# The last four gate outputs of the second token half, computed with the tokens stationary

## The chip, the cores and the metric

The kernel runs on one core of a Trainium2 chip. The metric is the device time of one execution in microseconds (us); lower is better. The profile calls the engines PE (TensorE, matmuls), PEld (the loading of its stationary operand, which overlaps PE), DVE (VectorE), ACT (ScalarE), POOL (GpSimd) and SP (the queue that issues DMAs here). SBUF is the on-chip memory with 128 partitions, PSUM the eight accumulation banks of 128 x 512 floats that PE writes.

## The reference

One layer of a hybrid decoder in float32, for one sequence of S = 1024 tokens and D = 1024 channels: an input projection with a pooling mixer and a gated recurrence, an output projection, an MLP with squared ReLU, and then a gated per-layer embedding (256 channels) and a final norm. Only the end matters here:

```python
z = rms_norm(h, norm_ple_g[l])
gate = jax.nn.sigmoid(z @ w_ple_gate[l] + b_ple_gate[l])
h = h + gate * (p[l] @ w_ple_proj[l])
return rms_norm(h, norm_final_g)
```

`rms_norm` divides each token's row by the root of the mean of its squares over the 1024 channels (plus 1e-6) and multiplies by a gain for each channel.

## The kernel before

Everything is held transposed: `H[o]` is a tile of 128 channels (partitions) by 1024 tokens, for o = 0 to 7. `FIRST` and `SECOND` are the first and second 512 tokens. Each float32 product is made of three matmuls over operands split into a high and a low part (`split`: ACT copies the high part, DVE subtracts it); in `mm` the stationary operand is a 128 x 128 block of weights and the tokens stream through as columns, taken in an interleaved order (`turns`; `got` and `by` undo it at the reading).

The gate stage is the end of the kernel. `GROUPS` names four groups of tokens, `ORDER` the outputs o in each: group 0 is `FIRST` with all eight outputs, group 1 is `SECOND` with outputs 2, 3, 4, 5, and groups 2 and 3 are the two halves of 256 tokens of `SECOND` with outputs 6, 7, 0, 1. For each output `ple_gate` makes 24 matmuls into one PSUM bank (8 blocks of channels, 3 products), `ple_proj` six into another (256 embedding channels), and `ple_out` reads both: sigmoid with the bias on ACT, multiply and add to `H[o]` on DVE, then the square on ACT (`Norm.add`) and its addition to an accumulator on DVE. `ple_psum` takes the two banks in turn from a pool of double banks (`banks`) and a pool of four single banks (`bank`, shared with the sums of the norms). The sums over channels for the final norm run over partitions, so they are matmuls with a matrix of ones (`Norm.sums`); `rstd` takes the root on ACT and the reciprocal on DVE. `finish` scales `H[o]` and stores four outputs at a time: the first half's during group 1, the 512:768 tokens' during group 3. The last 256 tokens end in `ple_last`: their outputs are scaled by the channel gain (`gain`) and transposed in 32 x 32 blocks on DVE (`turned`) so that the root of a token stands in a partition, and the last output's chain is written out step by step in cuts of 128 tokens, with three stores.

The weights of outputs 0 to 3 are loaded and split in the order of `FETCH` into two rotating pairs of tiles, so those of 0 and 1 are loaded again for the later groups; those of outputs 4 to 7 are split once, during group 0, into `B[4:]` in the space of `a_all`. `Z` (eight tiles, space "ple") holds the first half's normed and split tokens, `a_pair(k, 48)` the second half's.

The order on each engine comes from a planner: it places an instruction as soon as it takes its inputs to be ready, in program order among those that are. `pin`, while `in_order` is set, ties an instruction behind the one written before it on its engine; `ple_last` is pinned throughout. All DMAs of this stage go through SP's one queue, in order.

Of the kernel before, what the change touches and what calls it, by code (L numbers as in the profile page):

```python
# [7 lines left out]
F32 = mybir.dt.float32  # L8
# [5 lines left out]
P = 128  # L14
# [21 lines left out]
FRONT, BACK = (0, 1, 2, 3), (4, 5, 6, 7)  # L36
FETCH = ((0, 1, 2, 3), (), (0, 1), ())
# [21 lines left out]
def block_kernel(  # L59
# [4 lines left out]
    vec: bass.AP,  # L64
    w_lru: bass.AP,
# [42 lines left out]
    def pairs(tiles):  # L108
        return list(zip(tiles[::2], tiles[1::2]))
# [867 lines left out]
    Z, ple = [], []  # L977

    def open_ple():
        leave("s2")  # L980
        leave("wd")
        tiles = space("ple", 10, F32R)
        small[:] = tiles[8:]
        Z[:] = pairs(tiles[:8])
# [29 lines left out]
    gate_p, held = {}, []  # L1014
    root = pool.tile([P, 1], F32, name="root")
# [9 lines left out]

    def ple_gate(g, hs, o, pg, held=False):
        if o in FETCH[g]:
            gate_p[o] = weights()
        whi, wlo = gate_p[o]
        for k in range(NT):  # L1030
            zhi, zlo = z3(k, hs)
            mm(
                [(slice(0, hs.stop - hs.start), pg)], kblk(whi, k), kblk(wlo, k), zhi, zlo,
                k == 0, k == NT - 1, held=held and k == 0,
            )
# [18 lines left out]
    n_end = NT * (S - GROUPS[-1].start)  # L1054
    out_v = out[:, : NT * S - n_end].rearrange("p (o s) -> p o s", o=NT)
    out_end = out[:, NT * S - n_end :].rearrange("p (b x) -> p b x", b=n_end // S * 4)
    turned_all = t_all[:, 1:3].rearrange("p a s -> p (a s)").rearrange("p (b o j) -> p b o j", o=NT, j=32)
    turned_flat = t_all[:, 1:3].rearrange("p a s -> p (a s)").rearrange("p (b x) -> p b x", x=32 * NT)

    def store(os, hs):  # L1060
        nc.sync.dma_start(out_v[:, os, hs], h_all[:, os, hs])

    def finish(hs, os):

        if 0 in os:
            fin.rstd(rfin, fin.sums((hs,)))
        if hs != FIRST:
            for o in os[::4]:
                x = h_all[:, o : o + 4, hs]
                n = hs.stop - hs.start  # L1070
                nc.vector.tensor_tensor(x, x, rfin[:, hs].unsqueeze(1).broadcast_to([P, 4, n]), ALU.mult)
                store(slice(o, o + 4), hs)
            return
        for o in os:
            hv = H[o][:, hs]
            nc.vector.scalar_tensor_tensor(hv, hv, col("g_fin", o), rfin[:, hs], ALU.mult, ALU.mult)
            if o % 4 == 3:
                store(slice(o - 3, o + 1), hs)

    def gain(o, hs):  # L1080
        return nc.scalar.activation(H[o][:, hs], H[o][:, hs], AF.Identity, scale=col("g_fin", o))

    def turned(o, src=None):
        src = H[o][:, GROUPS[-1]] if src is None else src
        return nc.vector.transpose(turned_all[:, :, o], src)

    def ple_last(hs, prev, o, pg, pj):

        n = hs.stop - hs.start
        m = n // 2  # L1090
        t, e = (T[3 + i % 2][:, :n] for i in (o, o + 1))
        before, own = (T[3 + i][:, HALF : HALF + n] for i in range(2))
        scaled = T[3][:, HALF + n :][:, :n]
        hv = H[o][:, hs]
        cuts = slice(0, m), slice(m, n)
        in_order[:] = [True]
        pin(nc.scalar.activation(before, H[prev][:, hs], AF.Square))
        pin(gain(prev, hs))
        pin(nc.scalar.activation(by(t, pg), got(pg), AF.Sigmoid, bias=col("b_ple", o)))
        pin(nc.scalar.activation(root, t[:, :1], AF.Sqrt))  # L1100
        pin(turned(prev))
        pin(nc.vector.tensor_tensor(by(e, pj), by(t, pj), got(pj), ALU.mult))
        sums = [bank(f"n3_ps{hs.start}_{i}")[:, :m] for i in range(2)]
        for x, cut in zip(sums, cuts):
            for i, sq in enumerate((T[0][:, hs], before)):
                nc.tensor.matmul(x, ones_f, sq[:, cut], start=i == 0, stop=False)
        for x, cut in zip(sums, cuts):
            pin(nc.vector.tensor_tensor(hv[:, cut], hv[:, cut], e[:, cut], ALU.add))
            pin(nc.vector.tensor_tensor(own[:, cut], hv[:, cut], hv[:, cut], ALU.mult))
            nc.tensor.matmul(x, ones_f, own[:, cut], start=False, stop=True)  # L1110
        pin(nc.scalar.activation(scaled, hv, AF.Identity, scale=col("g_fin", o)))

        few = spread[:, 16:24]

        def roots(i):
            r = rfin[:, hs][:, cuts[i]]
            pin(nc.vector.transpose(r, sums[i]))
            x = few[:, 4 * i : 4 * i + 4]
            pin(nc.scalar.activation(x, r.rearrange("p (b t) -> p b t", t=32)[:, :, 0], AF.Sqrt, bias=eps, scale=1.0 / D))
            return x  # L1120

        def inverse(x):
            pin(nc.vector.reciprocal(x, x))

        def on_act(b):
            x = turned_flat[:, b]
            pin(nc.scalar.activation(x, x, AF.Identity, scale=few[:, b : b + 1]))

        def on_dve(b):
            x = turned_flat[:, b]  # L1130
            pin(nc.vector.tensor_scalar_mul(x, x, few[:, b : b + 1]))  # L1131

        def leave_for(bs):
            nc.sync.dma_start(out_end[:, bs], turned_flat[:, bs])

        a = roots(0)
        pin(turned(o, scaled))
        inverse(a)
        on_dve(0)
        on_act(1)  # L1140
        leave_for(slice(0, 2))
        b = roots(1)
        on_dve(2)
        on_act(3)
        leave_for(slice(2, 4))
        inverse(b)
        on_act(6)
        on_dve(4)
        on_dve(5)
        on_dve(7)  # L1150
        leave_for(slice(4, 8))
        in_order.clear()

    END = len(GROUPS) - 1
    for g, hs in enumerate(GROUPS):
        last = len(ORDER[g]) - 1
        if g == 1:
            fin.tmp = T[3:5]
        if g == END:
            fin.n[hs.start] = len(ORDER[1])  # L1160
        for n, o in enumerate(ORDER[g]):
            end = g == END and n == last
            pg, pj = ple_psum(g, hs, o, end)
            if g == 0 and n < 2:
                ple_gate(g, hs, o, pg, n == 1)
                held.append((o, pg, pj))
                if n == 0:
                    first_sums()
                    continue
                for o, pg, pj in held:  # L1170
                    ple_proj(hs, o, pj)
                for o, pg, pj in held:
                    ple_out(hs, o, pg, pj)
            elif end:
                ple_gate(g, hs, o, pg)
                ple_proj(hs, o, pj)
            else:
                ple_proj(hs, o, pj)
                if g == END and n == 1:
                    finish(GROUPS[END - 1], FRONT)  # L1180
                ple_gate(g, hs, o, pg)
            if g == 0 and 1 <= n < 5:
                raw = wp.tile([P, S], F32, tag="raw", name=f"wg0_{n + 3}_raw")
                nc.sync.dma_start(raw, w_gate[n + 3])
                split(raw, *B[n + 3])
                gate_p[n + 3] = B[n + 3]

            if (g > 0 or n > 1) and not end:
                ple_out(hs, o, pg, pj, g < END or n < last - 1)
# [7 lines left out]
            if g == 1:  # L1197
                gain(o, hs)
                finish(FIRST, DONE[n])
            if g == END - 1:  # L1200
                gain(o, hs)
                turned(ORDER[1][n])
            if g == END and n < last - 1:
                gain(o, hs)
                turned(o)
            if g == END and n == 1:
                finish(GROUPS[END - 1], BACK)
            if end:
                ple_last(hs, ORDER[g][n - 1], o, pg, pj)
    leave("ple")  # L1210
# [75 lines left out]
```

## Time and profile before

| what | value |
|---|---|
| median of 3 runs | 923.79 us (923.67 to 924.34) |
| the profiled execution | 923.81 us, of which 922.0 us are the span from first to last instruction |
| granted PE clock | 0.999 |
| PE busy | 914.2 us, 4357 matmuls |
| DVE busy | 760.3 us |
| ACT busy | 457.9 us |
| group 1 on PE | about 860.4 to 886.3 us |
| groups 2 and 3 on PE | about 886.3 to 913.5 us |
| from the last projection matmul to the end | about 8.5 us |

How to read the lines quoted below: a line of the timeline gives the start in us from the span's start, the duration, the engine, the line of the kernel, the operation, output<-input by the program's names, the shape and the count; the bracket tells how long the engine sat idle before it and what ended that. Lines merge instructions of one kind that follow one another. A line of the chain in order of time gives start, duration, engine and tile. A line of DMA issues gives output<-input, queue, count, size of each and the median us from issue to landing. A line of stretches gives the stretch, its length, the busy time of each engine with its instructions, the granted PE clock and the share of time in which DMA engines were busy. `ps_e` and `ps_j` are the PSUM banks of gate and projection (a double bank goes by `ps_e` alone).

### The profile page before, as it was taken

The numbers are of one execution on the slowest core, as the hardware profiler recorded it, in microseconds if no ns is written. First come the engines' busy times: TensorE is split into PE (matmuls) and PEld (weight loads), VectorE is DVE, ScalarE is ACT, GpSimd is POOL, SyncE is SP. The second block draws the span as 40 slices with busy tenths as digits, with TensorE's granted clock in tenths as the row PEclk, the third lists the DMA queues.
The fourth block names the chain that finished last, engine by engine and source line by source line (L and its number), as shares of the span: only waits on it lengthen the run. The fifth ranks groups of instructions, "written<-read, shape, count | busy, mean of one in ns | idle before, by whom it ended". The sixth has DMA issues, their size and how long they took to land.

```text
span 922.0 us, 11206 instructions
## 1 busy us (share of the span) xinstructions
PE 914.2 (99%) x4357; PEld 798.1 (87%) x4357; DVE 760.3 (82%) x911; ACT 457.9 (50%) x535; POOL 5.4 (1%) x7
## 2 busy tenths in 40 slices
PE   9999999999999999999999999999999999999997
PEld 7888888888888888888888888888888888888896
DVE  7997984669998888888888989979786669789575
ACT  7567892447543343344334554443443337455345
POOL 0000000002000000000000000000000000000000
PEclk9999999999999999999999999999999999999999
DMA  7210143111254355345534989366632341041022
GB/s 266 91 56 26 44 166 109 69 45 66 73 185 169 126 166 196 141 135 173 194 126 149 331 321 347 101 202 209 197 113 96 114 160 45 1 138 47 1 92 92
DMA packets 44900, 123.97 MB, mean 134 GB/s; under 512 B 4144, under 2 KB 6192, under 8 KB 44848
## 3 DMA queue, kind: packets, MB, share of 16 engines
q1 hardware_dynamic: 44704, 123.22, 38.7%
q8 instruction: 34, 0.56, 0.3%
q14 instruction: 18, 0.15, 0.1%
q10 hardware_dynamic: 144, 0.04, 0.0%
HBM read 89.69 MB, written 33.55 MB: 134 GB/s over the span
## 4 chain that ended last, share of the span: by engine, by line
PE 98%; DMA 1%; DVE 0%; SPq 0%; ACT 0%; issue 0%; DVEq 0%
PE ps_P_d L350 31%; PE ps_P_u L350 31%; PE ps_i L350 10%; PE ps_e L350 10%; PE ps_o L350 9%; PE ps_l L350 3%; PE ps_j L350 1%; PE ps_g L564 1%; DMA h<-in_xT 1%; PE ps_p L350 1%; PE n_ps L416 0%; PE n_ps L417 0%; DVE t L1131 0%; SPq L486 0%; DVE a L182 0%; ACT a L181 0%
## 5 line engine op out<-in xcount | busy, mean ns | idle before, releaser
L350 PE MATMUL ps_P_d<-a,wd_P_hi 128*128 128x512 f32 x880 | 261.7, 379 | 0.0
L350 PEld LDWEIGHTS ps_P_d<-a,wd_P_hi 128*128 128x128 f32 x880 | 166.3, 189 | 23.6
L350 PE MATMUL ps_P_d<-a,wd_P_lo 128*128 128x512 f32 x440 | 166.8, 379 | 0.0
L350 PE MATMUL ps_P_u<-a,wu_hi 128*128 128x512 f32 x512 | 152.3, 379 | 0.0
L350 PE MATMUL ps_P_u<-y,wu_hi 128*128 128x512 f32 x384 | 114.2, 379 | 0.0
L350 PEld LDWEIGHTS ps_P_u<-a,wu_hi 128*128 128x128 f32 x512 | 96.8, 189 | 13.8
L350 PE MATMUL ps_P_u<-a,wu_lo 128*128 128x512 f32 x256 | 97.0, 379 | 0.0
L350 PEld LDWEIGHTS ps_P_d<-a,wd_P_lo 128*128 128x128 f32 x440 | 83.2, 189 | 11.8
L350 PEld LDWEIGHTS ps_P_u<-y,wu_hi 128*128 128x128 f32 x384 | 72.6, 189 | 10.4
L740 DVE TENSOR_TENSOR t<-t,ps_P_u 128x512 f32<-128x512 f32 (+1 forms) x80 | 62.6, 782 | 20.4 <-PE ps_P_u L350 20.4
L350 PE MATMUL ps_i<-a,wi_hi 128*128 128x512 f32 x288 | 74.4, 380 | 0.0
L350 PE MATMUL ps_P_u<-y,wu_lo 128*128 128x512 f32 x192 | 72.8, 379 | 0.0
L178 ACT ACTIVATE a<-wd 128x1024 fp32r<-128x1024 f32 x56 | 58.7, 1053 | 21.9 <-DMA wd<-act 13.1
L179 DVE TENSOR_TENSOR a<-wd,a 128x1024 fp32r<-128x1024 f32 x56 | 67.3, 1221 | 1.0 <-ACT a L178 0.6
L350 PE MATMUL ps_o<-y,wo_hi 128*128 128x512 f32 x256 | 65.7, 379 | 0.0
L350 PEld LDWEIGHTS ps_i<-a,wi_hi 128*128 128x128 f32 x288 | 54.1, 189 | 8.8 <-issue 1.0
L178 ACT ACTIVATE wu_hi<-wu 128x1024 fp32r<-128x1024 f32 x24 | 25.4, 1058 | 69.8 <-PE ps_P_u L350 44.1
L178 ACT ACTIVATE wu_hi<-wu_raw 128x1024 fp32r<-128x1024 f32 (+1 forms) x26 | 25.2, 974 | 66.3 <-PE ps_P_u L350 41.3
L350 PEld LDWEIGHTS ps_o<-y,wo_hi 128*128 128x128 f32 x256 | 48.4, 189 | 6.8
L350 PEld LDWEIGHTS ps_P_u<-a,wu_lo 128*128 128x128 f32 x256 | 48.4, 189 | 6.8
L178 ACT ACTIVATE wd_P_hi<-wd 128x1024 fp32r<-128x1024 f32 x24 | 25.3, 1054 | 50.0 <-PE ps_P_d L350 50.0
L740 DVE TENSOR_TENSOR h<-h,ps_P_d 128x512 f32<-128x512 f32 (+1 forms) x40 | 31.6, 789 | 19.0 <-PE ps_P_d L350 19.0
(238 smaller groups left out, 1504.9 us busy)
## 6 DMA issues: line engine op xcount, KB each, us to landing
wd<-act SPq DMA_DIRECT2D x56, 512.0 KB, 5.8
act<-t SPq DMA_DIRECT2D x32, 512.0 KB, 4.4
wu_raw<-in_w_up SPq DMA_DIRECT2D x16, 512.0 KB, 3.6
wu<-in_w_up SPq DMA_DIRECT2D x16, 512.0 KB, 4.2
act<-wu SPq DMA_DIRECT2D x16, 512.0 KB, 4.8
wd<-in_w_down SPq DMA_DIRECT2D x16, 512.0 KB, 6.0
h<-in_xT SPq DMA_DIRECT2D x14, 512.0 KB, 4.6
wg_raw<-in_w_gate SPq DMA_DIRECT2D x10, 512.0 KB, 3.3
```

The source lines that it names most:

```text
L178: first = pin(nc.scalar.activation(hi, src, AF.Copy))
L179: lowest[:] = [pin((eng or nc.vector).tensor_tensor(lo, src, f32(hi), ALU.subtract)).ins]
L350: ins = nc.tensor.matmul(ps, w, turns(z[:, hs]), start=first and z is zhi and w is whi, stop=last and w is wlo, skip_group_check=more,)
L564: nc.tensor.matmul(x, w[r, o * P : (o + 1) * P], turns(z[r, at : at + HALF]), start=n == 0, stop=n == 2)
L740: (eng or nc.vector).tensor_tensor(to, to if y is None else y, x, ALU.add)
```

## The change

Groups 2 and 3 go. Group 1 keeps 512 tokens and now has the outputs 2, 3, 0, 1. The outputs 4 to 7 of the second half are computed in four blocks of 128 tokens (`NTOK`): the tokens of a block are the stationary operand, the weights of all four outputs stream as 512 columns, and a block's result has tokens in the partitions and 512 channels along the row. For that the split weights of outputs 4 to 7 lie interleaved in two tiles (`quad`), so that block k of all four outputs is one row of 512.

What belongs to a block of tokens must then lie along rows too. The residual of outputs 4 to 7 (before the gate) and the finished values of outputs 0 to 3 are transposed in 32 x 32 blocks on DVE (`turn_block`), stored to DRAM in four DMAs for each half of the channels and each 256 tokens (`turn_out`, pieces of 512 bytes) and loaded back as rows of tokens (`turn_in`, 2 KB for each partition). The gain and the bias come along rows in one new input that is broadcast to all partitions. The mean of squares runs along the row: `mean` is one DVE instruction that multiplies and reduces, with the earlier part as its starting value.

For blocks 0 to 2 `token_out_all` adds the bias (DVE), takes the sigmoid (ACT), multiplies by the projection and adds the residual (DVE); `early_half` squares and scales outputs 0 to 3 of a block (block 0 does it for blocks 0 and 1); `token_finish` reduces the other half, takes root and reciprocal, scales the two halves on ACT and DVE and stores 512 KB. For block 3 `token_last` does it in two cuts of 256 channels, pinned, with two stores. The squares of the second half no longer go through the accumulator and the ones matmuls. `finish` only serves the first half, spread over group 1 and block 0.

```diff
-GROUPS = (slice(0, 512), slice(512, 1024), slice(512, 768), slice(768, 1024))
-ORDER = ((0, 1, 2, 3, 4, 5, 6, 7), (2, 3, 4, 5), (6, 7, 0, 1), (6, 7, 0, 1))
-DONE = ((), (0, 1, 2, 3), (4, 5), (6, 7))
-FETCH = ((0, 1, 2, 3), (), (0, 1), ())
+GROUPS = (slice(0, 512), slice(512, 1024))
+ORDER = ((0, 1, 2, 3, 4, 5, 6, 7), (2, 3, 0, 1))
+DONE = ((), (0, 1, 2), (3, 4), (5,), (6, 7), (), (), ())
+FETCH = ((0, 1, 2, 3), (0, 1))
+NTOK = 4
+NQUAD = 4 * P
...
-        B[4:] = [a_pair(i, 64) for i in range(4, NT)]
+        quad[:] = [
+            a_all[:, n + 64 : n + NT * NQUAD + 64].rearrange("p (k x) -> p k x", k=NT)
+            for n in (NT * S, NT * S + NT * NQUAD)
+        ]
...
+    bounce = [
+        [dram.tile([8, 32, 4, P], F32, name=f"turn{half}_{j}") for j in range(2)] for half in range(2)
+    ]
+    def turn_block(o, j):
+        to = late[NTOK + 2 * (o // 4) + j].rearrange("p (b o x) -> p b o x", o=4, x=32)
+        n = HALF + 256 * j
+        nc.vector.transpose(to[:, :, o % 4], H[o][:, n : n + 256])
+    def turn_out(half, j):
+        src = late[NTOK + 2 * half + j].rearrange("p (b x) -> p b x", x=P)
+        for g in range(4):
+            nc.sync.dma_start(
+                bounce[half][j][:, :, g].rearrange("b t x -> t b x"), src[32 * g : 32 * g + 32]
+            )
+    def turn_in(half, i):
+        b = 4 * (i % 2)
+        nc.sync.dma_start(
+            quarter(i, half), bounce[half][i // 2][b : b + 4].rearrange("b t g x -> (b t) (g x)")
+        )
+    def mean(i, x, before, to):
+        nc.vector.tensor_tensor_reduce(
...
+            x, x, 1.0 / D, before, ALU.mult, ALU.add, ms[:, to : to + 1],
+        )
+    def early_half(i):
+        x = quarter(i, 0)
+        mean(i, x, EPS, 4 * i)
+        nc.vector.tensor_tensor(x, x, g_row[:, :NQUAD], ALU.mult)
+    def token_gate(i, pg):
+        for k in range(NT):
+            zhi, zlo = z3(k, token_slice(i))
+            for n, (z, w) in enumerate(((zhi, quad[0]), (zhi, quad[1]), (zlo, quad[0]))):
+                nc.tensor.matmul(
+                    pg, z, turns(w[:, k]), start=k == n == 0, stop=k == NT - 1 and n == 2
+                )
+    def token_out_all(i, pg, pj):
+        t, e = T[3 + i % 2][:, FIRST], T[3 + i % 2][:, SECOND]
+        whole = slice(0, NQUAD)
+        nc.vector.tensor_tensor(by(t, pg), got(pg), by(b_row, pg), ALU.add)
+        nc.scalar.activation(t, t, AF.Sigmoid)
+        nc.vector.tensor_tensor(by(e, pj), by(t, pj), got(pj), ALU.mult)
+        late_half(i, e, whole)
+    def root_of(i):
+        r = ms[:, 4 * i + 3 : 4 * i + 4]
+        pin(nc.scalar.activation(r, ms[:, 4 * i + 2 : 4 * i + 3], AF.Sqrt))
+        pin(nc.vector.reciprocal(r, r))
+        return r
+    def token_finish(i):
+        mean(i, quarter(i, 1), ms[:, 4 * i : 4 * i + 1], 4 * i + 2)
+        r = root_of(i)
+        x, y = quarter(i, 0), quarter(i, 1)
+        nc.scalar.activation(x, x, AF.Identity, scale=r)
+        nc.vector.scalar_tensor_tensor(y, y, r, g_row[:, NQUAD:], ALU.mult, ALU.mult)
+        nc.sync.dma_start(token_out[:, i], late[i])
+    def token_last(i, pg, pj):
+        t, e = T[3 + i % 2][:, FIRST], T[3 + i % 2][:, SECOND]
+        cuts = slice(0, 256), slice(256, NQUAD)
+        in_order[:] = [True]
+        for a, cut in enumerate(cuts):
+            pin(nc.vector.tensor_tensor(t[:, cut], got(pg)[:, a], b_row[:, cut], ALU.add))
+            pin(nc.scalar.activation(t[:, cut], t[:, cut], AF.Sigmoid))
+        pin(nc.scalar.activation(root, t[:, -1:], AF.Sqrt))
...
+        for a, cut in enumerate(cuts):
...
+            pin(nc.vector.tensor_tensor(by(e[:, cut], x), by(t[:, cut], x), got(x), ALU.mult))
...
+            pin(nc.vector.tensor_tensor(yv, yv, ev, ALU.add))
+            pin(
+                nc.vector.tensor_tensor_reduce(
...
+        r = root_of(i)
...
+        for cut in cuts:
...
+            pin(nc.scalar.activation(x, x, AF.Identity, scale=r))
+            pin(nc.vector.scalar_tensor_tensor(v, v, r, g_row[:, NQUAD:][:, cut], ALU.mult, ALU.mult))
+            nc.sync.dma_start(token_out[:, i].rearrange("p (h x) -> p h x", h=2)[:, :, cut], both[:, :, cut])
...
+        if g == 1:
+            leave("ple")
+            late[:] = space("late", 8, F32)
...
+                for j in range(2):
+                    turn_block(o, j)
+                if n < 2:
+                    for x in range(4, NT):
+                        turn_block(x, n)
+                    turn_out(1, n)
+                    for i in range(2):
+                        turn_in(1, 2 * n + i)
+                if n == 3:
+                    for j in range(2):
+                        turn_out(0, j)
+                        for i in range(2):
+                            turn_in(0, 2 * j + i)
+                finish(DONE[n])
+                if n == 1:
+                    nc.sync.dma_start(row[:, : S + NQUAD], rows.broadcast_to([P, S + NQUAD]))
+    for i in range(NTOK):
+        end = i == NTOK - 1
+        pg, pj = ple_psum(2, slice(0, NQUAD), i, end)
+        if end:
+            token_gate(i, pg)
+            pj = [x[:, :256] for x in (pj, bank("ps_j_end"))]
+            for a, x in enumerate(pj):
+                token_proj(i, x, slice(256 * a, 256 * a + 256))
+            token_last(i, pg, pj)
+            continue
+        token_proj(i, pj, slice(0, NQUAD))
+        token_gate(i, pg)
+        token_out_all(i, pg, pj)
+        for x in ((0, 1), (2,), (3,))[i]:
+            early_half(x)
+        token_finish(i)
+        finish(DONE[4 + i])
```

More of the change, by code (lines that the diff above doesn't have):

```diff
@@ L64, in block_kernel @@
     vec: bass.AP,
+    rows: bass.AP,
     w_lru: bass.AP,
@@ L1052, in ple_out @@
             fin.add(H[o], hs)
[L1054 to L1061, printed above, removed]
@@ L1063, in finish @@
-    def finish(hs, os):
-        if 0 in os:
[L1066 to L1073, printed above, removed]
+    first_out = out[:, : NT * HALF].rearrange("p (o s) -> p o s", o=NT)
+    token_out = out[:, NT * HALF :].rearrange("p (i x) -> p i x", i=NTOK)
@@ L1080, in gain @@
[L1080 to L1095, printed above, removed]
-        in_order[:] = [True]
[L1097 to L1151, printed above, removed]
```

104 lines of the change are left out of this document (61 added, 43 removed).

## The prediction

> **What bounds the kernel now.** I read the page's shares and its chain first, then the stretches of the gate stage (last outputs of the second 512 tokens), then the order of work there and behind the last matmul.
>
> ```profile
> span 922.0 us, 11206 instructions
> PE 98%; DMA 1%; DVE 0%; SPq 0%; ACT 0%; issue 0%; DVEq 0%
> ```
>
> TensorE carries the chain; nothing else counts unless it holds TensorE up or lies behind its last matmul. The stretches, with the busy time of each engine:
>
> ```profile
> core 0: us, PE busy (x) PEld busy (x) DVE busy (x) ACT busy (x) POOL busy (x), PEclk, DMA share, GB/s
> 860.40:886.30 25.90, 25.90 (x122) 22.65 (x121) 18.70 (x30) 12.25 (x16) 0.00 (x0) 1.00 0.16 58
> 886.30:913.50 27.20, 27.20 (x245) 27.20 (x244) 16.16 (x35) 14.98 (x29) 0.00 (x0) 1.00 0.18 62
> 913.50:922.00 8.50, 1.86 (x12) 1.29 (x11) 4.20 (x15) 3.80 (x8) 0.00 (x0) 0.87 0.32 123
> ```
>
> The second row is group 1 of the order (four outputs, 512 tokens), the third the last four outputs in two groups of 256 tokens, the fourth the tail. TensorE never waits in the middle two, and the granted clock is full. So two things can change: how long TensorE works from 886.3 on, and what lies behind it. The rows that price both:
>
> ```profile
> 879.82 1.46 PE L350 MATMUL ps_e<-proj,proj 128*128 128x512 f32 x6
> 881.11 5.34 PE L350 MATMUL ps_e<-a 128*128 128x512 f32 x24
> 886.29 0.83 PE L350 MATMUL ps_j<-proj,proj 128*128 128x256 f32 x6
> ...
> 889.64 0.83 PE L350 MATMUL ps_e<-proj,proj 128*128 128x256 f32 x6
> ...
> 903.87 0.12 PE n_ps L416
> ...
> 912.66 0.83 PE L350 MATMUL ps_j<-proj,proj 128*128 128x256 f32 x6
> ...
> 916.67 1.91 SPq L1134 DMA_DIRECT2D out<-t  x3
> ...
> 917.29 0.88 DVE L1131 TENSOR_SCALAR t<-t,edge 128x256 f32<-128x256 f32 x3
> ```
>
> (The short row is from the chain in order of time.) Start to start, six projection matmuls of 512 columns take 1.29 and 24 gate matmuls 5.18: 6.47 us for an output. With 256 columns an output takes 3.35.
>
> **The change, part by part.** *TensorE.* Removed: eight times 3.35 and two sum matmuls of 0.12: 27.04, from 886.29 to 913.33. Added: four blocks of 128 tokens, each 6 + 24 matmuls of 512 columns. Tokens and weights change places, so count, contraction and columns are those of the 512-column rows: 4 x 6.47 = 25.88, and 0.05 because the last projection is cut into two times six of 256 (2 x 0.67 for 1.29). TensorE ends at 912.22, 1.11 earlier. In the last block the gate goes first and ends at 886.29 + 3 x 6.47 + 5.18 = 910.88. PSUM doesn't hold it: the last block's third bank is freed by the first read of the block before it, some 5 us earlier. Group 1 has the same size in another order (2, 3, 0, 1), its refetched weights come in the same order as now.
>
> *Work in front of the blocks.* Sixteen DVE transposes of 128x256 at 0.44 replace two of the present ones inside group 1: about 6.2 us more on a DVE with 18.7 busy of 25.9, less two additions of squares (the form of 0.69, below) that go. It fits, and the transposes of outputs 4 to 7 need no result of group 1. Were the cover gone, it would delay only the weight split for the fourth output, which has 5 us to spare. The SP queue gets 24 bounce transfers and one broadcast at 0.46 each, 11.5 us, in a stretch where it issued nothing between the rows
>
> ```profile
> 837.68 0.33 SPq L196 DMA_DIRECT2D wg_raw<-in_w_gate  x1
> 880.98 29.40 SPq L1061 DMA_DIRECT2D out<-h  x4
> ...
> 2.59 1.38 SPq L486 DMA_DIRECT2D h<-in_xT  x3
> ```
>
> Splitting the weights into interleaved columns handles the same 128x1024 elements; I cost it at nothing, under TensorE.
>
> *The bounce of outputs 0 to 3.* Its last member, output 1, is the last of group 1; its chain is the present one of output 5:
>
> ```profile
> 886.49 0.69 ACT L1048 ACTIVATE t<-ps_e,vecs 128x512 f32<-128x512 f32 x1 [0.27 <-PE ps_e L350]
> 887.21 0.69 DVE L1049 TENSOR_TENSOR t<-t,ps_e 128x512 f32<-128x512 f32 x1 [0.52 <-ACT t L1048]
> 887.94 0.69 DVE L1050 TENSOR_TENSOR h<-h,t 128x512 f32<-128x512 f32 x1
> ...
> 884.72 0.44 DVE L1085 STREAM_TRANSPOSE t<-h 128x256 f32<-128x256 f32 x1
> ...
> wd<-act SPq DMA_DIRECT2D x56, 512.0 KB, 5.8
> act<-t SPq DMA_DIRECT2D x32, 512.0 KB, 4.4
> wg_raw<-in_w_gate SPq DMA_DIRECT2D x10, 512.0 KB, 3.3
> out<-t SPq DMA_DIRECT2D x2, 256.0 KB, 2.1
> out<-t SPq DMA_DIRECT2D x1, 512.0 KB, 2.7
> ```
>
> The sum of output 1 stands at 888.63, its first transpose at 889.1; four stores go out at 0.46, the last at 890.5. No row shows a store in 512-byte pieces: 2.1 (256 KB alone) and 4.4 (512 KB among other traffic) bound it; I take 2.7, the quiet 512 KB, since the four together are that. The loads wait on SP for it: 893.2. For the load the ends are 2.1 and 5.8 (this kernel's own reload from DRAM, busy queue); I take 3.3, the quiet load. Block 0 has its early half at 896.5.
>
> *The chain of a block.* Between blocks DVE and ACT must do: add bias, sigmoid, multiply, add residual, square and reduce, root, reciprocal, scale. Sigmoid and Sqrt need different tables:
>
> ```profile
> 906.39 0.31 ACT L431 ACTIVATE edge<-t,eps 128x8 f32<-128x8 f32 x1
> 906.61 0.49 ACT L1081 ACTIVATE h<-h,vecs 128x256 f32<-128x256 f32 x1
> ...
> 907.12 1.28 ACT L1048 ACT_TABLE_LOAD   x1
> 908.41 0.47 ACT L1048 ACTIVATE t<-ps_e,vecs 128x256 f32<-128x256 f32 x1
> ...
> 877.66 0.72 ACT L1081 ACTIVATE h<-h,vecs 128x512 f32<-128x512 f32 x1
> ...
> 838.88 0.75 DVE L920 SCALAR_TENSOR_TENSOR t<-h,vecs,rstd 128x512 f32<-128x512 f32 x1
> 839.54 0.68 DVE L1050 TENSOR_TENSOR h<-h,t 128x512 f32<-128x512 f32 x1
> ...
> 822.08 1.22 DVE L179 TENSOR_TENSOR wg_lo<-wg_raw,wg_hi 128x1024 fp32r<-128x1024 f32 x1
> ...
> 915.59 0.30 ACT L1119 ACTIVATE edge<-t,eps 128x4 f32<-128x4 f32 x1 [0.18 <-DVE t L1117]
> 915.92 0.18 DVE L1123 RECIPROCAL edge<-edge 128x4 f32<-128x4 f32 x1
> 916.13 0.51 ACT L1127 ACTIVATE t<-t,edge 128x256 f32<-128x256 f32 x1 [0.24 <-DVE edge L1123]
> ```
>
> The load stands behind the scaling, and the next sigmoid behind the load. The load of Sqrt's table hides beside DVE's three operations. No row shows multiply-and-reduce. Its ends are 0.69 (plain, 512) and 1.22 (twice the elements); I take 0.85, near the 0.75 of the three-operand form with something for writing the sum (256: 0.55). Steps from one sigmoid to the next: 0.72 + 0.73 + 0.72 + 0.90 (reduce and hand-over) + 0.33 + 0.21 + 0.72 + 1.29 (load) = 5.62, under TensorE's 6.47. A late block is thus never caught up by more than 0.85 per block, and one that is late by more passes it on to the last.
>
> Block 0: read from 892.96 (TensorE 892.76 + 0.20), residual added at 895.8; then DVE waits for the data at 896.5, and two early halves (blocks 0 and 1) stand before its own reduction: 2 x (0.76 + 0.60) = 2.7, so 899.2. Root at 900.1, reciprocal at 900.7 (block 1's bias add takes DVE first), scaling to 901.6, load, sigmoid of block 1 at 902.9. Plus twice 5.62: the last block's sigmoid at 914.15; its bias add and sigmoid are written to stand behind block 2's scaling on both engines. That is where the lead goes: the gate of the last block could be read at 911.1. The early halves of blocks 2 and 3 (1.36 each) lie in DVE's idle 1.4 while ACT loads.
>
> *Tail.* The 256-column steps of the present blocks:
>
> ```profile
> 893.19 0.47 ACT L1048 ACTIVATE t<-ps_e,vecs 128x256 f32<-128x256 f32 x1 [0.86 <-PE ps_e L350]
> 893.70 0.42 DVE L1049 TENSOR_TENSOR t<-t,ps_e 128x256 f32<-128x256 f32 x1 [1.46 <-ACT t L1048]
> 894.15 0.43 DVE L1050 TENSOR_TENSOR h<-h,t 128x256 f32<-128x256 f32 x1
> ```
>
> From the sigmoid: 0.51 to the first multiply, two cuts of multiply, add, reduce at 0.45 + 0.45 + 0.55: 3.4; root and reciprocal 0.54; two scalings of 0.47 and 0.51: last store at 919.05. Before, the last store left at 918.2 with 2.7 to land; now 256 KB lands in 2.1, so 3.2 from issue to the end in place of 3.8. End 922.25, 0.25 later than 922.0. The execution took 923.81 (median of the runs 923.79): 924.1.
>
> [...] The load is 1.28 between 907.12 and the sigmoid at 908.41. [...]
>
> Two f32 inputs cost a three-operand instruction no rate: 0.75 against 0.69. [...]
>
> **The rivals.** *Slower, the bounce is late (0.24).* Place: DVE waiting for block 0's early half. It decides from 895.8 on; each microsecond behind 896.5 is one at the end. With 4.4 and 5.8, the kernel's own rows for a round trip, data come at 890.5 + 4.4 + 5.8 = 900.7: 4.2 later, 928.3. An order on SP or DVE that waits for one transfer before issuing the next gives 1.5 to 3. For it: SP is one queue in order, and a 1 MB store of the first half stands near it. Against: the queue is else quiet.
>
> *Slower, the reduction runs at half rate (0.12).* 0.37 more: twice for the early halves, three times in the chain, 0.35 twice where the early halves outgrow the idle time, 0.14 twice in the tail: 2.8, so 926.9.
>
> *Faster (0.14).* The planner puts the next sigmoid before the scaling, so the backlog of block 0 is gone when block 2 is read at 905.90. Then 0.72 + 5.62 gives the last sigmoid at 912.24, the end at 920.3: 922.2. Only with a plain 0.69 for the reductions does it come under 921.9. Against: the last block is tied to block 2's scaling.
>
> **How the numbers follow.** A measurement tells about 0.2% (1.85 us) from no change. The forecast, a TensorE gain eaten by the chain of the blocks, 0.50, has its own range of 922.2 to 925.6. Slower holds 0.24 + 0.12, faster 0.14. The range is 922.0 to 927.5: it takes in the half-rate reduction and most of the late bounce and leaves out the full round trip.
>
> **What would show it.** 30 matmuls in 6.47 per block without a wait, TensorE's last matmul near 912.2; DVE idle before the first reduction, released by a DMA; a table load between scaling and sigmoid in each block; the last sigmoid near 914, three after the gate's end. Wrong, if the early half lands after 898, if the reductions take other than 0.85, or if TensorE waits in the blocks.

## The result and the profile after

The changed kernel takes 926.12 us (median of 9 runs, 925.73 to 926.76) where the kernel before takes 923.83 (9 runs, 923.38 to 924.98): ratio 1.0024, 95% interval 1.0013 to 1.0034. It is slower by a quarter of a per cent, 2.3 us. The forecast was 924.1, no change; its range of 922.0 to 927.5 holds the result. The profiled spans are 923.9 and 922.0; the profiled execution of the changed kernel took 925.73, the shortest of the nine.

The page of the changed kernel, first line and chain, still says nothing but TensorE:

```profile
span 923.9 us, 10987 instructions
...
PE 98%; DVE 1%; issue 0%; ACT 0%; ACTq 0%
```

The same three stretches show where the time went (columns as before: PE, PEld, DVE, ACT, POOL, clock, DMA share, GB/s):

```profile
860.40:886.30 25.90, 25.90 (x121) 22.67 (x120) 20.69 (x39) 8.19 (x10) 0.00 (x0) 1.00 0.58 174
886.30:913.50 27.20, 25.91 (x126) 22.66 (x124) 16.77 (x37) 8.58 (x13) 0.00 (x0) 1.00 0.42 122
913.50:923.90 10.40, 0.00 (x0) 0.00 (x0) 4.85 (x14) 5.12 (x9) 0.00 (x0) 0.64 0.36 134
```

Group 1 keeps TensorE full, with the transposes under it. The blocks keep TensorE busy for 25.91 in place of 27.20. Everything lost lies behind. TensorE's order of work, the first block, the start of the second, and the end:

```profile
886.10 1.46 PE L1135 MATMUL ps_j<-proj,proj 128*128 128x512 f32 x6
...
892.57 1.46 PE L1135 MATMUL ps_e<-proj,proj 128*128 128x512 f32 x6
...
911.37 0.83 PE L1135 MATMUL ps_j_end<-proj,proj 128*128 128x256 f32 x6
```

No bracket: no wait. A block is 6.47 (886.10 to 892.57), and the last matmul ends at 912.2. DVE and ACT in the blocks, in that order (on DVE, what is left out is work, but for one gap of 0.27 at 913.1; on ACT it has waits too):

```profile
894.89 0.69 DVE L1143 TENSOR_TENSOR late<-late,t 128x512 f32<-128x512 f32 x1
899.25 0.69 DVE L1148 TENSOR_TENSOR t<-ps_e,t 128x512 f32<-128x512 f32 x1 [3.67 <-PE ps_e L1126]
899.86 0.68 DVE L1109 CUSTOM_DVE_ANT_0 t<-late 128x512 f32<-128x512 f32 x1
...
903.66 0.75 DVE L1109 CUSTOM_DVE_ANT_0 t<-late,edge 128x512 f32<-128x512 f32 x1
...
905.73 0.69 DVE L1148 TENSOR_TENSOR t<-ps_e,t 128x512 f32<-128x512 f32 x1 [1.30 <-PE ps_e L1126]
906.33 0.15 DVE L1156 RECIPROCAL edge<-edge 128x1 f32<-128x1 f32 x1
906.40 0.67 DVE L1109 CUSTOM_DVE_ANT_0 t<-late 128x512 f32<-128x512 f32 x1
...
907.00 0.75 DVE L1164 SCALAR_TENSOR_TENSOR late<-late,edge,t 128x512 f32<-128x512 f32 x1
907.66 0.68 DVE L1117 TENSOR_TENSOR late<-late,t 128x512 f32<-128x512 f32 x1
908.27 0.75 DVE L1109 CUSTOM_DVE_ANT_0 t<-late,edge 128x512 f32<-128x512 f32 x1
908.94 0.08 DVE L1109 DVE_READ_ACCUMULATOR2_ANT edge<- 128x1 f32 x1
...
913.97 0.75 DVE L1173 TENSOR_TENSOR t<-ps_e,t 128x256 f32<-128x256 f32 x2
```

```profile
899.98 0.63 ACT L1149 ACTIVATE t<-t 128x512 f32<-128x512 f32 x1 [5.84 <-DVE t L1148]
...
904.46 0.20 ACT L1155 ACTIVATE edge<-edge 128x1 f32<-128x1 f32 x1 [2.55 <-DVE edge L1109]
906.49 1.28 ACT L1149 ACT_TABLE_LOAD   x1 [1.83 <-DVE edge L1156]
907.79 0.63 ACT L1149 ACTIVATE t<-t 128x512 f32<-128x512 f32 x1
908.33 0.71 ACT L1163 ACTIVATE late<-late,edge 128x512 f32<-128x512 f32 x1
909.05 1.28 ACT L1155 ACT_TABLE_LOAD   x1
910.35 0.20 ACT L1155 ACTIVATE edge<-edge 128x1 f32<-128x1 f32 x1
...
914.47 1.28 ACT L1174 ACT_TABLE_LOAD   x1 [0.44 <-DVE t L1173]
915.76 0.72 ACT L1174 ACTIVATE t<-t 128x256 f32<-128x256 f32 x2
```

DVE ends block 0's half at 895.6 and then stands idle for 3.67, waiting for TensorE and not for a DMA: block 1's bias add (L1148, 899.25) has been put ahead of block 0's early half (899.86). Yet the data were there at about 896: SP issues the loads from 893.06 on, and they land in 2.9 (median of four):

```profile
893.06 0.82 SPq L1103 DMA_DIRECT2D late<-turn  x2
```

```profile
turn<-late SPq DMA_DIRECT2D x8, 128.0 KB, 2.5
late<-turn SPq DMA_DIRECT2D x4, 256.0 KB, 2.9
```

So block 0's root comes at 904.46, and its reciprocal, again behind a bias add (block 2's, after 1.30 of idle), at 906.33. From 905.73 on DVE has next to no gap, and on that stretch lie block 0's reciprocal and scaling, block 2's early half and block 1's reduction: 0.07 + 0.66 + 1.21 + 0.67 = 2.6 us, from each start to the next, that belong ahead of it. The last bias add comes at 913.97, the last sigmoid at 915.76.

### The profile page after: what moved, and what is told of

Same layout as the page of the kernel before. It is cut to its first block, busy times and chain, and to the rows that moved or that the text cites. A ratio compares the mean times of both kernels' runs of the same rounds, so it can differ in the third digit from the quotient of the medians.

```text
span 923.9 us, 10987 instructions
## 1 busy us (share of the span) xinstructions
PE 911.2 (99%) x4229; PEld 792.4 (86%) x4229; DVE 763.7 (83%) x921; ACT 449.0 (49%) x514; POOL 5.6 (1%) x7
## 4 chain that ended last, share of the span: by engine, by line
PE 98%; DVE 1%; issue 0%; ACT 0%; ACTq 0%
PE ps_P_u L352 31%; PE ps_P_d L352 31%; PE ps_i L352 10%; PE ps_o L352 9%; PE ps_e L352 8%; PE ps_l L352 3%; PE ps_e L1126 2%; PE ps_j L352 1%; PE ps_g L566 1%; PE ps_p L352 1%; PE ps_l L482 0%; PE ps_j L1135 0%; DVE t L1109 0%; PE n_ps L418 0%; PE n_ps L419 0%
```

## The experiments

The table has all kernels. The last column runs from the start of the last six projection matmuls (911.37 in the changed kernel) to the end of the span; it leaves out that these six start up to 0.1 us earlier or 0.8 later than in the changed kernel, from one profiled execution to another. The kernel before has 9.34 there (922.0 - 912.66).

| kernel | median, us | ratio to before (95%) | span | from last six matmuls |
|---|---|---|---|---|
| changed kernel | 926.12 | 1.0024 (1.0013 to 1.0034) | 923.9 | 12.53 |
| e1_order | 923.86 | 1.0000 (0.9991 to 1.0009) | 921.9 | 10.45 |
| e2_last_first | 922.69 | 0.9989 (0.9980 to 0.9998) | 920.8 | 9.19 |
| e3_no_root | 924.29 | 1.0003 (0.9994 to 1.0012) | 922.4 | 10.77 |
| e4_early_data | 923.99 | 1.0003 (0.9994 to 1.0012) | 921.9 | 10.44 |
| e5_early_moved | 926.06 | 1.0026 (1.0016 to 1.0035) | 924.3 | 12.58 |
| e6_recip_moved | 925.89 | 1.0021 (1.0012 to 1.0030) | 924.1 | 12.45 |
| e7_load_moved | 922.74 | 0.9988 (0.9979 to 0.9996) | 920.7 | 9.21 |
| e8_root_ahead | 924.34 | 1.0002 (0.9992 to 1.0011) | 922.1 | 10.60 |
| e9_both_loads | 921.68 | 0.9974 (0.9963 to 0.9985) | 919.9 | 8.20 |
| e10_own_tiles | 921.69 | 0.9976 (0.9966 to 0.9987) | 920.4 | 8.20 |
| e11_no_extra | 924.06 | 1.0003 (0.9993 to 1.0012) | 921.9 | 10.67 |
| e12_tiles_alone | 925.65 | 1.0019 (1.0010 to 1.0028) | 924.0 | 12.16 |

The orders are given as words with the number of the block: `add` bias add, `sig` sigmoid, `prod` multiply, `resid` residual added (`mult` is both), `square` and `gain` the two halves of `early_half` (`early` is both), `mean` the block's reduction, `sqrt`, `recip`, `scale` (ACT) and `stt` (DVE) the two scalings. Each engine keeps its own words in the order written.

**The order by hand.** On DVE the early halves and the reduction stand where their data are, each root ahead of the next sigmoid.

```diff
-add0 sig0 prod0 resid0 add1 sig1 square0 prod1 gain0 square1 resid1 gain1 mean0 sqrt0
-add2 sig2 recip0 scale0 square2 stt0 gain2 mean1 sqrt1 prod2 square3 resid2
-recip1 scale1 gain3 stt1 mean2 sqrt2 recip2 scale2 stt2
+add0 sig0 mult0 early0 early1 mean0 sqrt0 add1 sig1 recip0 scale0 stt0
+mult1 early2 mean1 sqrt1 add2 sig2 recip1 scale1 stt1
+early3 mult2 mean2 sqrt2 recip2 scale2 stt2
```

> The blocks' DVE and ACT instructions are tied in an order written out by hand: both early halves and block 0's reduction stand ahead of block 1's bias add, reciprocal and scaling of a block ahead of the next block's multiply. Nothing else changes. Theory (DVE stood idle 3.67 us at 895.6 and 1.30 us at 904.4 because a bias add that waits for TensorE was placed in front of work that was ready): the early halves start near 896, block 2's chain then runs from its own read at 905.7, the last sigmoid goes from 915.76 to about 913.5 and the span from 923.9 to about 921.7, 0.3 under before. Rival (the data of the bounce really come late, the order only shows it): the early halves still start near 899, span 923.5 to 924. Rival (the table loads set the pace of the chain whatever the order): span not under 923.

Span 921.9: the order is worth 2.0 us. The forecast's end, 922.25, is close to this, though by another way (below). DVE and ACT of this kernel:

```profile
895.90 0.69 DVE L1109 CUSTOM_DVE_ANT_0 t<-late 128x512 f32<-128x512 f32 x1 [0.24 <-DMA late<-turn]
...
905.80 0.69 DVE L1262 TENSOR_TENSOR t<-ps_e,t 128x512 f32<-128x512 f32 x1 [0.84 <-PE ps_e L1126]
```

```profile
900.88 0.63 ACT L1264 ACTIVATE t<-t 128x512 f32<-128x512 f32 x1
...
904.99 0.20 ACT L1279 ACTIVATE edge<-edge 128x1 f32<-128x1 f32 x1 [1.57 <-DVE edge L1109]
...
907.87 0.63 ACT L1264 ACTIVATE t<-t 128x512 f32<-128x512 f32 x1
...
912.44 1.28 ACT L1174 ACT_TABLE_LOAD   x1 [0.43 <-DVE t L1173]
913.73 0.72 ACT L1174 ACTIVATE t<-t 128x256 f32<-128x256 f32 x2
```

The first reduction now waits 0.24 for a DMA, as forecast, and block 1 has its root at 904.99, ahead of block 2's bias add.

**The last block first.** The order by hand, with the last block's bias adds and sigmoids ahead of block 2's root, reciprocal and scalings.

```diff
-early3 mult2 mean2 sqrt2 recip2 scale2 stt2  (then token_last)
+early3 mult2 mean2  (in token_last: sqrt2 behind the sigmoids, recip2 and scale2 ahead of the second reduction, stt2 behind it)
```

> As the run with the order by hand, and the last block's two bias adds and sigmoids stand ahead of block 2's root and scaling, so that one table load for Sqrt serves the last two blocks. Theory (what is left after the order is the tie of the last block to block 2's scaling and the table load behind it): the last sigmoid comes at about 911.4, right behind the gate's end, the span falls to about 919.5, which is 4.4 under the changed kernel and 2.5 under before: faster by about 0.27%. Rival (the tail is set by the work behind the last matmul, which is the same): within 0.5 us of the run with the order by hand.

The last sigmoid comes at 911.66, 2.1 earlier than in the order by hand, but only 1.1 to 1.3 us reach the end; the theory's 919.5 was 1.3 too early. Two things are seen to take the rest. Block 2's scaling now lies between the last sigmoid and the last scaling: 915.62 - 911.66 = 3.96, against 917.38 - 913.73 = 3.65. And its 512 KB store leaves just ahead of the last two of 256 KB, which take 3.0 to land (first row, this kernel) where they took 2.3 (second, order by hand):

```profile
out<-late SPq DMA_DIRECT2D x2, 256.0 KB, 3.0
```

```profile
out<-late SPq DMA_DIRECT2D x2, 256.0 KB, 2.3
```

**No root.** The changed kernel without a table load behind 886.

```diff
-        pin(nc.scalar.activation(r, ms[:, 4 * i + 2 : 4 * i + 3], AF.Sqrt))
+        pin(nc.scalar.activation(r, ms[:, 4 * i + 2 : 4 * i + 3], AF.Identity))
...
-        pin(nc.scalar.activation(root, t[:, -1:], AF.Sqrt))
```

> The changed kernel with Identity in place of Sqrt for the roots of the four blocks, and without the early Sqrt that only loads the table: the root is left out, and with it every table load from block 0 on. The planner's order stays as it is for the early halves. Theory (of the loads only the one ahead of the last sigmoid lies on the path, 1.28, with 0.4 of waiting ahead of it): span 922.2 to 922.6. Rival (each of the loads between blocks lies on the path): three loads, 3.9 less, span near 920.

Span 922.4, inside the theory's numbers; the 1.8 us in the last column are nearly as much as the order gives. They are not the same microseconds: DVE comes to the last bias add at 913.74, hardly earlier than 913.97, so its late work is still there. What is gone is the load between that add and the last sigmoid, and 0.5 us along the way (TensorE 0.26 later in this run).

**Early data.** Outputs 0 to 3 are loaded from the other half's bounce, stored long before.

```diff
-            quarter(i, half), bounce[half][i // 2][b : b + 4].rearrange("b t g x -> (b t) (g x)")
+            quarter(i, half), bounce[1][i // 2][b : b + 4].rearrange("b t g x -> (b t) (g x)")
```

> The changed kernel, but the early halves are loaded from the bounce of outputs 4 to 7, which is in DRAM some 20 us earlier: the values of outputs 0 to 3 are replaced by those of the residual of 4 to 7. All transfers and instructions stay. Theory (the early halves are late by their place in the order, not by the transfer): they move ahead of block 0's end, both idle stretches go, and the span is that of the run with the order by hand, 921.8, not lower, since block 2's own chain with two table loads then sets the end. Rival (the bounce's own duration costs): lower than the run with the order by hand by 1 us or more.

With the data early the planner itself puts block 0's early half, root and scaling ahead of block 1's bias add, and the time is that of the order by hand, which has the true bounce. So the bounce's own duration costs nothing: what cost was an order made as if the data came later than 895.9. That this is what the planner reckoned with is inferred from the two orders; its own figure is not in the profile.

**One idle stretch at a time.** In e5_early_moved the early halves and block 0's reduction go ahead of block 1's bias add, on DVE alone; in e6_recip_moved block 0's reciprocal and DVE scaling go ahead of block 2's bias add. In the latter block 0's outputs 0 to 3 are stored before they are scaled.

```diff
 e5:
-add0 sig0 prod0 resid0 add1 sig1 square0 prod1 gain0 square1 resid1 gain1 mean0 sqrt0 add2
+add0 sig0 prod0 resid0 square0 gain0 square1 gain1 mean0 add1 sig1 sqrt0 prod1 resid1 add2
 e6:
-add2 sig2 recip0 scale0 square2 stt0 gain2
+recip0 stt0 add2 sig2 scale0 square2 gain2
```

> The order of the changed kernel on every engine, except that on DVE the early halves of blocks 0 and 1 and block 0's reduction go ahead of block 1's bias add (so the idle 3.67 us at 895.6 is used). Theory (only the last of the waits in the chain counts): DVE will then have nothing left when block 1 is done near 902 and will wait for the gate of block 2, behind which block 0's reciprocal still stands: 906.33 as before, and everything behind it as in the changed kernel, span 923.9, the same time. Rival (the largest idle stretch is the one that costs): the 2 us come back, span near 921.9 as with the whole order written by hand.

> The order of the changed kernel on every engine, except that on DVE block 0's reciprocal and its scaling go ahead of block 2's bias add (so the idle 1.30 us at 904.4 is used), the early halves staying where they are. Theory: the reciprocal stands at 904.7 and DVE's work behind 905.73 is 0.73 us shorter (0.07 of the reciprocal's pitch, 0.66 of the scaling); but the root of block 1 stands behind ACT's load, which the order on ACT still puts at 909.05 to 910.35, so DVE will wait for it a little: 0.2 to 0.7 us of the 2.0 come back, span 923.2 to 923.7. Rival (this wait alone is the whole loss): span near 921.9. Rival (the early halves are the whole loss): span 923.9.

DVE of the first:

```profile
906.07 0.69 DVE L1262 TENSOR_TENSOR t<-ps_e,t 128x512 f32<-128x512 f32 x1 [3.67 <-PE ps_e L1126]
906.68 0.15 DVE L1296 RECIPROCAL edge<-edge 128x1 f32<-128x1 f32 x1
```

The 3.67 us of idle only moved, to the front of block 2's bias add, and nothing came back. The second, with DVE and then ACT:

```profile
905.17 0.75 DVE L1302 SCALAR_TENSOR_TENSOR late<-late,edge,t 128x512 f32<-128x512 f32 x1
906.01 0.69 DVE L1262 TENSOR_TENSOR t<-ps_e,t 128x512 f32<-128x512 f32 x1
...
910.87 0.16 DVE L1296 RECIPROCAL edge<-edge 128x1 f32<-128x1 f32 x1 [0.23 <-ACT edge L1294]
```

```profile
909.34 1.28 ACT L1294 ACT_TABLE_LOAD   x1
910.63 0.20 ACT L1294 ACTIVATE edge<-edge 128x1 f32<-128x1 f32 x1
```

The idle time is used (0.75 us of scaling now ahead of 906.01), but DVE then waits for block 1's root, which ACT makes at 910.63 behind its load. 0.1 us came back, less than the 0.2 to 0.7 expected.

**Block 1's root ahead of block 2.** Both moves together, and with them block 2's early half and block 1's reduction and root.

```diff
+add0 sig0 prod0 resid0 square0 gain0 square1 gain1 mean0 add1 sig1 sqrt0
+prod1 resid1 recip0 stt0 square2 gain2 mean1 sqrt1 add2 sig2 scale0 recip1 stt1
+scale1 square3 gain3 prod2 resid2 mean2 sqrt2 recip2 scale2 stt2
```

> The early halves of blocks 0 and 1 ahead of block 1's bias add and block 0's reciprocal ahead of block 2's, which singly brought back 0.0 and 0.1 us, and with them block 1's own reduction and root ahead of block 2's bias add and sigmoid; block 1's sigmoid still ahead of block 0's root and block 0's scaling on ACT still behind block 2's sigmoid, as in the changed kernel. Theory (the 2 us are a block's root standing one block late: what counts is only whether block 1's root is done before DVE turns to block 2 at 905.7): root of block 1 at 905.0, reduction of block 2 near 910.0, last sigmoid at 913.7, span 921.9, as with the order written by hand. Rival (the order on ACT in the earlier blocks counts as well): span 922.5 to 923.9.

Span 922.1, between theory and rival, but 10.60 in the last column against 10.45 for the order by hand: of the 2.1 us all but 0.15 are back. The rest is seen at ACT's order, which puts two scalings ahead of block 2's root: DVE waits 0.47 for that root, where the order by hand waits 0.27.

**The load in front of a sigmoid.** In the order by hand the load for the last sigmoid starts only when the first bias add of the last block is done (912.44). One more sigmoid of 128x1, behind block 2's root, gives the load something earlier to go with (e7); one more behind block 1's root does it for block 2 (e9).

```diff
 e7:
-early3 mult2 mean2 sqrt2 recip2 scale2 stt2
+early3 mult2 mean2 sqrt2 warm2 recip2 stt2  (scale2 in token_last, behind the sigmoids)
 e9, against e7:
-mult1 early2 mean1 sqrt1 add2 sig2 recip1 scale1 stt1 early3 mult2 mean2 sqrt2 warm2 recip2 stt2
+mult1 early2 mean1 sqrt1 warm1 square3 add2 sig2 recip1 scale1 stt1 mult2 mean2 gain3 sqrt2 warm2 recip2 stt2
+            keep(nc.scalar.activation(root, ms[:, 4 * i + 2 : 4 * i + 3], AF.Sigmoid))  # warm
```

> The order by hand (span 921.9, last sigmoid at 913.73 behind a table load of 1.28 that began only when the last block's bias add was done), with one more sigmoid of 128x1 right behind block 2's root, so that the load has something to go with that waits for no DVE work, and ACT's scaling of block 2 behind the last block's sigmoids. Theory (a load starts with the wait of the activation it was placed for): load from 911.05 to 912.33, last sigmoid at 912.6 in place of 913.73, everything behind it 1.1 us earlier, span 920.8, 922.7 us. Rival (the load runs ahead of the wait anyway, and the last sigmoid was late for another cause): span 921.9, 923.9 us. Rival (the tail is set by block 2's store, which now goes 1.5 us later): span 921.9 or more.

> The kernel with the moved load (span 920.7), with one more small sigmoid behind block 1's root too, so that the load for block 2's sigmoid also runs while DVE still waits for the gate, and block 3's first reduction put into DVE's idle time before block 2's bias add. Theory (a load starts with the wait of the activation it was placed for, and that is the last 1.3 us by which block 2 is behind its gate): block 2's sigmoid at 906.5 in place of 907.9, its reduction done by 909.6 in place of 910.8, the last bias add waits for the gate alone (911.0), last sigmoid at 911.5 in place of 912.5, span 919.7, 921.7 us. Rival (behind the gate's end DVE's own work is the bound, 5.2 us of it between 905.8 and 911.0): the last sigmoid is no earlier than 912.2, span 920.4 or more.

ACT of the first and then of the second kernel:

```profile
911.10 1.28 ACT L1291 ACT_TABLE_LOAD   x1
...
912.51 0.71 ACT L1174 ACTIVATE t<-t 128x256 f32<-128x256 f32 x2
```

```profile
905.24 1.28 ACT L1291 ACT_TABLE_LOAD   x1
...
906.84 0.63 ACT L1267 ACTIVATE t<-t 128x512 f32<-128x512 f32 x1
...
911.69 0.75 ACT L1174 ACTIVATE t<-t 128x256 f32<-128x256 f32 x2 [0.22 <-DVE t L1173]
```

The two steps bring 1.2 and 1.0 us in the last column, where 1.1 and 1.0 were expected (the first with block 2's scaling on ACT moved as well, the second with the two halves of block 3's `early_half`). The last sigmoid of the second stands at 911.69, right behind the gate's end, and this kernel is faster than both: 921.68, ratio 0.9974.

**Why the load waits.** A sigmoid of the last two blocks has two things to wait for: DVE's bias add, and ACT's own earlier use of its tile, since two tiles serve four blocks in turn. That the number of waits decides where the load starts is the author's theory and was not shown: the profile does not tell on which instruction a wait was put. What the runs show is where the loads start with shared and with separate tiles.

The tile taken for the last block holds the row of gains, so values are scaled by something else; the work is the same. e10 is e9 without its extra sigmoids and with a tile for each block; e11 is e9 without the extra sigmoids and with the shared tiles; e12 is the changed kernel with the tiles alone.

```diff
-        t, e = T[3 + i % 2][:, FIRST], T[3 + i % 2][:, SECOND]
+        t, e = (T[3], T[4], T[0], T[1])[i][:, FIRST], (T[3], T[4], T[0], T[1])[i][:, SECOND]
```

> The kernel with both loads moved (span 919.9), without its two extra sigmoids, and with tiles of its own for each block's gate in place of two tiles in turn, so that the last two blocks' sigmoids have no second wait (on ACT's own earlier use of the tile) beside that on DVE. Theory (with two waits the one on DVE is put on the table load, with one it stays on the sigmoid): both loads run while DVE is still at work, last sigmoid at 911.6, span 919.9, 921.7 us. Rival (only the extra sigmoid moved the loads): last sigmoid near 913.9, span 922.0, 924 us.

> The kernel with both loads moved (span 919.9) without its two extra sigmoids, the gates in two tiles in turn as in the changed kernel. Theory: both loads wait for DVE again, 1.0 us at block 2's sigmoid and 1.3 at the last: last sigmoid at 913.9, span 922.0, 923.9 us. Rival (the order alone gave the gain, the loads nothing): span 919.9 to 920.4.

> The changed kernel with nothing but a tile of its own for each block's gate; the order on DVE and ACT stays. Theory (in this order DVE works without a gap from 905.7 to 914.7, so a load moved ahead pays only at the last sigmoid, where it can start at 914.0 instead of 914.47): span 923.4, 925.6 us. Rival (the loads are the loss): span 921.9.

The loads of the first, of the second and of the third kernel, one fence for each:

```profile
905.90 1.28 ACT L1267 ACT_TABLE_LOAD   x1
907.28 0.63 ACT L1267 ACTIVATE t<-t 128x512 f32<-128x512 f32 x1
...
910.48 1.28 ACT L1174 ACT_TABLE_LOAD   x1
```

```profile
912.38 1.28 ACT L1174 ACT_TABLE_LOAD   x1 [1.64 <-DVE t L1173]
913.68 0.72 ACT L1174 ACTIVATE t<-t 128x256 f32<-128x256 f32 x2
```

```profile
905.13 1.28 ACT L1149 ACT_TABLE_LOAD   x1
...
914.50 1.28 ACT L1174 ACT_TABLE_LOAD   x1
```

e10 and e11 differ in the tiles alone. With tiles of their own the loads start right behind the roots, and the time is that of e9 (921.69); with shared tiles 2.5 us are lost again in the last column (10.67 for 8.20), so without the loads the rest of e9's order brings nothing over the order by hand (10.45). In the planner's order (e12) the loads run ahead too, block 2's right behind block 0's root and the last right behind block 2's scaling, but this brings only 0.4 in the last column, near the 0.5 expected: from block 2's bias add (906.19) to the last one (914.43) DVE has no wait but one of 0.27.

## Why the prediction was right or wrong

**TensorE: right.** 6.47 for a block, no wait, the last matmul at 912.2. Group 1 hid the transposes and the bounce's issues, with DVE at 20.69 of 25.90.

**The bounce: right, a little too dear.** Loads forecast to go out at 893.2 went at 893.06; data forecast for 896.5 came at 895.9 (the first reduction of the order by hand). The first rival, in its main form, is refuted: the early data changed nothing that the order did not.

**Reductions: mis-sized.** Priced at 0.85, they take 0.69 and 0.75 with a 0.08 read of the accumulator behind them; from their start to the next instruction's it is 0.60 to 0.67 back to back and up to 0.78 elsewhere. The prediction named "other than 0.85" as a sign that it is wrong, and here it was. The second rival is refuted: 0.69 is the time of a plain addition of that size. No run shows the half rate that it reckoned with; its 0.37 over 0.85 would make 1.22, the row with twice the elements, and the runs showed 0.67 to 0.75 in its place.

**Block 0: the step that failed.** The forecast had DVE wait for the data at 896.5 and do the two early halves at once, block 1's bias add going ahead only of the reciprocal; root at 900.1. In the changed kernel block 1's bias add stood ahead of the early halves too, though ready only at 899.2, and the root came at 904.46. An order on DVE that waits stood in the first rival, but as waiting for a transfer, and priced at 1.5 to 3 us with no row behind it; it waited for TensorE, and the order by hand shows its price: 2.0 in the span, 2.1 in the last column.

**"One that is late passes it on": half right.** The root was 4.4 late and the last sigmoid only 1.6 (915.76 for 914.15), so 2.75 was caught up in two blocks and not at most 1.7, because block 1's sigmoid did not wait for the root as the forecast had it: 899.98 in place of 902.9. What reached the end went through DVE: the 2.6 us of earlier blocks' work that stood behind 905.73, less 0.5 by which the order by hand takes longer from start to start behind its own 905.80. Up to the last bias add DVE needs 8.24 in the changed kernel and 6.14 in the order by hand. Filling either idle stretch alone brought 0.1 at most.

**Chain: near in sum, by luck.** The forecast's 914.15 and 922.25 are close to the 913.73 and 921.9 of the order by hand, but not by its chain. There block 1's sigmoid stood at 900.88 and not at 902.9, and DVE waited 0.84 for TensorE ahead of block 2 (905.80): nothing of block 0's lateness was left. The time came back at two places: block 2's sigmoid stood at 907.87, 2.07 and not 0.72 behind that, its load having started only behind the bias add; and the step to the last sigmoid was 5.86 for 5.62.

**Loads: right in size, wrong in place.** A load of 1.28 did stand in front of the last two sigmoids of the changed kernel. It was not through the scaling ahead of it: block 2's sigmoid (907.79) went ahead of a scaling (908.33), and in e11, where blocks share a tile, the load ahead of the last sigmoid waited 1.64 for DVE (912.38), in e10, where they do not, it started at 910.48 without a wait. Behind that scaling, which ends at 909.04, the load for Sqrt starts at 909.05 and the root at 910.35: 1.3 in all.

**Tail: right.** 8.1 from the last sigmoid to the end, and it is 923.9 - 915.76 = 8.14.

**The sum: in the range by its width.** The result, 926.12, lies outside the 922.2 to 925.6 that the forecast gave as its own, and inside the range that was widened for a half-rate reduction and a late bounce. Neither happened as it was priced, so that the range holds the result is mostly luck. Of the signs that the prediction named, TensorE's came. DVE's idle stretch ahead of the first reduction was ended by TensorE and not by a DMA, block 1's sigmoid had no load ahead of it and block 2's had the scaling behind it, and the last sigmoid was at 915.76, not near 914. Of the 2.0 us by which the forecast missed, 1.65 are in the profiled span: the order's 2.0, less the 0.35 by which the forecast's end was later than that of the order by hand. The other 0.37 are spans too: every execution takes 1.7 to 1.9 more than its span, as forecast, but the median one has a span of 924.3, and the profiled one is the shortest. What made the others longer was not traced.

**The faster rival: its condition came true, its time did not.** The next sigmoid did go ahead of the scaling (899.98 and 907.79, the first scaling at 908.33), yet DVE's backlog was not gone at 905.73, and the last sigmoid came at 915.76 in place of 912.24. In the order by hand the backlog was gone, and the last sigmoid still came at 913.73, 1.5 behind the rival's. With the loads out of the way as well (e9) the last sigmoid is at 911.69 and the end at 919.9, against the rival's 920.3.

## What to carry to other kernels

When an engine's order is chosen by estimates of when data come, look in the trace for an engine that idles on one input while another, queued behind it, is already there. Price it by what it pushes behind the last input, not by the length of the gap: here 3.67 us of idle were worth nothing alone, and the order as a whole 2.0. Where a function's table must be switched on the path to the end, look whether the load starts with the data: here a tile of its own for the activation behind the switch, or a tiny activation of the same table earlier, brought it forward, worth 2.5 us for two loads.

## What had not been expected of the hardware

Table loads started well ahead of their sigmoid's data in some of these kernels; e10 and e11, where they did and did not, differ in the tiles alone. With a tile for each block, block 2's load started right behind ACT's work before (905.90 in e10, DVE's add at 906.55, the sigmoid at 907.28); with a tile shared by two blocks it started only behind that add (906.35 in e11, the add at 905.58), and all of its 1.28 us came behind the data. With a tiny sigmoid ahead, moving the last one was worth 1.2 us (e7 against e1); with separate tiles, both together 2.5 (e10 against e11).

A multiply-and-reduce of 128x512 cost about what an addition cost in the changed kernel: 0.68 in the mean of four and, with the earlier part as its starting value, 0.75 in the mean of three, against 0.68 to 0.69. Back to back, the next instruction started together with the 0.08 read of the sum, 0.60 to 0.67 behind the reduction's start.

Two stores of 256 KB, the first 0.6 us behind a 512 KB store, landed in 3.0 in place of 2.3 (e2 and e1, one profiled execution each).
